# A written order for TensorE's projections and block products in a four-layer hybrid decoder trunk

## The chip, the cores and the metric

One core of a Trainium2 chip runs the whole network in one launch: 256 tokens, 1024 features, four layers, all in 32-bit floats. The metric is the device time of that launch in microseconds. The core has five engines that run side by side, each with its own in-order queue: TensorE (PE, with its weight loads PEld), VectorE (DVE), ScalarE (ACT), GpSimd (POOL) and SyncE (SP, which issues most DMAs).

## What is computed

Each layer is a half-weighted SwiGLU feed-forward network (FFN), a token mixer beside a memory attention, and a second FFN. The mixer is retention in layers 0 and 3, sparse attention with an indexer in layer 1, and native sparse attention in layer 2. Cut to what matters here:

```python
def swiglu(x, wg, wu, wd):
    return (jax.nn.silu(x @ wg) * (x @ wu)) @ wd     # wg, wu: 1024 x 2816, wd: 2816 x 1024

for i in range(DEPTH):
    h = rms_norm(x, ffn_norm[i, 0])
    x = x + 0.5 * swiglu(h, ffn_w_gate[i, 0], ffn_w_up[i, 0], ffn_w_down[i, 0])
    ...
    x = x + jnp.concatenate([y_mix, y_mem], axis=-1) @ w_out[i]
    h = rms_norm(x, ffn_norm[i, 1])
    x = x + 0.5 * swiglu(h, ffn_w_gate[i, 1], ffn_w_up[i, 1], ffn_w_down[i, 1])
```

## The kernel before

The tokens are two tiles of 128 rows (t = 0 and 1). Weights come from memory in units of 1 MB pieces (`raw`, three buffers). Every operand is split in two, a high half `hi` on ACT (line 264) and the rest `lo` on DVE (line 265), into nine slots each (`HALVES`), and one product is three matmuls: high by high, high by low, low by high. `mm3` (lines 290 to 294) writes these three. `project` (line 296) makes a projection from eight groups of them; half way through it calls `tick` (line 310), which splits some more weights and runs what is due. Delayed pieces, such as the transposes of the hidden activations `h` (`turn`, lines 1259 to 1264), are handed to `later` (line 348) with a number of ticks.

An FFN has eleven gate-and-up units and six down units, in the order of `FFN_ORDER`: g0 to g3, d0, g4, g5, d1, g6, g7, d2, g8, g9, d3, g10, d5, d4. A gate-and-up unit gives `pg`, from it `h`, and from its transposed halves (`hTh`, `hTl`) and the down weights the sums `acc`, over the whole FFN in four banks.

Units 4 and 5 go together, and so do 8 and 9: `joint` (line 460) computes their four block products for both token tiles with seven instead of eight, on sums and differences of weights (`t1` to `t4`; `b11`, `b21`, `b22` are plain) and of activations. Three PSUM banks A, B (both named `pg`) and C (`pj`) take them. There are 16 such blocks: two in each of eight FFNs. Of their seven products the last three and the vector work around them matter below:

```python
product(B, both("s3"), "t3", False)          # fourth
nc.vector.tensor_add(s3, B, s1)              # L493: reads bank B
product(A, half(1), "b21", False)            # fifth
chains[0].send((A, n0))                      # activation of A
nc.vector.tensor_sub(s3, C, s3)              # L496: reads bank C
product(B, both("a22"), "t4", False)         # sixth: adds to bank B
nc.vector.tensor_add(s1, B, s1)              # L498
chains[1].send((s1, n0)); chains[1].send((s3, n0))
product(C, both("s4"), "b22", False)         # seventh: adds to bank C
```

Behind a block stands the next down unit, d1 or d3, for tile 0 and then tile 1. [...]

Of the kernel before, what the change touches and what calls it, by code (L numbers as in the profile page):

```python
# [80 lines left out]
class Net:  # L81
    def __init__(self, ctx, tc, a, layers):
        self.tc, self.nc, self.a = tc, tc.nc, a
        self.layers = layers

        def pool(name, **k):
            return ctx.enter_context(tc.tile_pool(name=name, bufs=1, **k))

        self.cp, self.wp, self.ap, self.sp = pool("const"), pool("weights"), pool("act"), pool("small")
        self.ps = pool("psum", space=PSUM)  # L90
        self.units, self.raw, self.parts = [], {}, {}
        self.n_fetch = self.n_split = 0
        self.seq, self.due, self.queue, self.memkv = [], [], [[], []], {}
        self.ticks = 0
        self.jobs, self.open = [], []
        self.extra = []
        self.st, self.splits = [{}, {}], []
        self.plan()
# [188 lines left out]
        self.split()  # L287


    def mm3(self, out, ah, al, bh, bl, start, stop):  # L290
        mm = self.nc.tensor.matmul
        mm(out, ah, bh, start=start, stop=False)  # L292
        mm(out, ah, bl, start=False, stop=False)  # L293
        mm(out, al, bh, start=False, stop=stop)  # L294
# [53 lines left out]
    def later(self, n, fn, t=None):  # L348

        todo = [fn]  # L350

        def once():
            while todo:
                todo.pop()()

        self.due.append((n, once, t))
        return once
# [102 lines left out]
    def joint(self, u, chains):  # L460

        nc = self.nc
        while self.extra:
            self.extra.pop(0)()
        parts, ops = self.parts[u], self.ops
        s0 = self.st[0]["s"]
        both = lambda n: (ops[n][:, 0], ops[n][:, 1])
        half = lambda b: (s0[0][:, 4 * b:4 * b + 4], s0[1][:, 4 * b:4 * b + 4])

        def product(bank, a, name, first):  # L470
            mm = nc.tensor.matmul
            for k in range(4):
                bh, bl = [x[:, k % 2 * 512:k % 2 * 512 + 512] for x in parts[name][k // 2]]
                mm(bank, a[0][:, k], bh, start=first and k == 0, stop=False, skip_group_check=True)
                mm(bank, a[0][:, k], bl, start=False, stop=False, skip_group_check=True)
                mm(bank, a[1][:, k], bh, start=False, stop=k == 3, skip_group_check=True)
                if k == 1:
                    self.tick()

        n0 = self.st[0]["n"]  # L480
        A = self.pB("pg")
        product(A, half(0), "b11", True)
        s1 = self.t2([128, 512], "s1")
        nc.scalar.activation(s1, A, AF.Copy)
        B = self.pB("pg")
        product(B, both("s2"), "t2", True)
        s2 = self.t2([128, 512], "s2")
        nc.vector.tensor_add(s2, B, s1)
        C = self.bank("pj", "C")
        product(C, both("s1"), "t1", True)  # L490
        product(B, both("s3"), "t3", False)
        s3 = self.t2([128, 512], "s3")
        nc.vector.tensor_add(s3, B, s1)  # L493
        product(A, half(1), "b21", False)
        chains[0].send((A, n0))
        nc.vector.tensor_sub(s3, C, s3)  # L496
        product(B, both("a22"), "t4", False)
        nc.vector.tensor_add(s1, B, s1)  # L498
        chains[1].send((s1, n0))
        chains[1].send((s3, n0))  # L500
        product(C, both("s4"), "b22", False)
        nc.vector.tensor_sub(s2, C, s2)
        chains[0].send((s2, n0))
# [1090 lines left out]
```

## Time and profile before

| | before |
|---|---|
| median of the 3 runs shown | 2109.56 us (2107.13 to 2119.91) |
| profiled execution | 2109.68 us |
| its span in the trace | 2107.9 us |
| PE busy | 2028.5 us, 96% |
| DVE busy | 1520.9 us, 72% |
| ACT busy | 1114.2 us, 53% |
| POOL busy | 227.7 us, 11% |
| mean granted clock of TensorE | 0.985 |

The span runs from the first instruction to the last; 1.8 us lie around it. A busy PE is one with a matmul under way: matmuls overlap, so a row's duration is longer than the distance to the next row, and it is this distance that tells the rate. A row of a timeline ends, in brackets, with the idle time of its engine just before it and with what ended that.

### The profile page before, as it was taken

Reading aid. Unit: us, or ns where it says so; the run is one execution under the profiler, and the core shown is the slowest. Engines: PE = TensorE matmul, PEld = TensorE weight load, DVE = VectorE, ACT = ScalarE, POOL = GpSimd, SP = SyncE. Lnnn points to the kernel's source line nnn. Section 1 sums busy time; section 2 is a strip of 40 time slices with the busy share of each in tenths; the row PEclk is TensorE's granted clock in tenths of the full one; section 3 lists DMA queues with packets and bytes.
Section 4 is the critical chain, followed back from the end, with each engine's and each line's share of the span. In section 5 each row is a group of like instructions: output and inputs, shape, how many; then the busy total and the mean of one; then the engine's idle time right before and its main releaser. Section 6 shows DMA issues by size and latency. Waiting matters only on the chain.

```text
span 2107.9 us, 25369 instructions
## 1 busy us (share of the span) xinstructions
PE 2028.5 (96%) x9486; PEld 1628.5 (77%) x9486; DVE 1520.9 (72%) x2209; ACT 1114.2 (53%) x1562; POOL 227.7 (11%) x349
## 2 busy tenths in 40 slices
PE   8899999899989999989998999999899989999899
PEld 6677777778867887868777788877788778778687
DVE  7677757778767787867777876667786868658675
ACT  6455655446545555545545554544555545545453
POOL 0100411100100022100000112210000100301000
PEclk9999999999999999999999999999999999999999
DMA  7855535865683533684577443137744774436843
GB/s 260 261 189 220 180 120 200 241 218 200 213 245 143 205 110 120 234 246 145 218 235 242 182 173 130 64 121 235 241 179 180 231 248 181 159 120 215 249 149 126
DMA packets 66988, 402.11 MB, mean 191 GB/s; under 512 B 7600, under 2 KB 8016, under 8 KB 28080
## 3 DMA queue, kind: packets, MB, share of 16 engines
q1 hardware_dynamic: 56304, 364.54, 47.2%
q0 software_dynamic: 9408, 33.97, 8.3%
q10 hardware_dynamic: 1152, 1.97, 0.3%
q8 instruction: 75, 1.23, 0.2%
q14 instruction: 49, 0.40, 0.1%
HBM read 399.40 MB, written 1.05 MB: 190 GB/s over the span
## 4 chain that ended last, share of the span: by engine, by line
PE 74%; DMA 12%; DVE 8%; ACT 3%; issue 2%; POOL 1%; SPq 0%; ACTq 0%; DVEq 0%; POOLq 0%
PE pg L292 8%; PE pg L294 8%; PE pg L293 8%; PE acc L293 7%; PE acc L294 6%; PE acc L292 6%; DMA sum<-gu 5%; DVE lo L237 4%; DMA raw<-gu 3%; PE p L292 3%; DMA raw<-dn 3%; PE p L293 3%; PE p L294 3%; DVE lo L265 2%; PE pT L1262 2%
## 5 line engine op out<-in xcount | busy, mean ns | idle before, releaser
L265 DVE TENSOR_TENSOR lo<-raw,hi 128x1024 fp32r<-128x1024 f32 (+3 forms) x516 | 615.6, 1217 | 175.1 <-ACT hi L264 168.5
L264 ACT ACTIVATE hi<-raw 128x1024 fp32r<-128x1024 f32 (+3 forms) x516 | 527.1, 1046 | 273.0 <-DMA raw<-gu 79.0
L292 PE MATMUL pg<-hi,sh 128*128 128x512 f32 x896 | 354.8, 396 | 4.4 <-ACT hi L1347 3.4
L293 PE MATMUL pg<-lo,sh 128*128 128x512 f32 x896 | 350.7, 391 | 0.7 <-DVE lo L1348 0.7
L294 PE MATMUL pg<-hi,sl 128*128 128x512 f32 x896 | 349.8, 390 | 0.0
L292 PE MATMUL acc<-hi,hTh 128*128 128x512 f32 x704 | 286.0, 410 | 34.9 <-ACT hi L264 34.9
L293 PE MATMUL acc<-lo,hTh 128*128 128x512 f32 x704 | 288.0, 413 | 4.6 <-DVE lo L265 4.4
L294 PE MATMUL acc<-hi,hTl 128*128 128x512 f32 x704 | 282.4, 405 | 0.0
L236 ACT ACTIVATE hi<-sum 128x1024 fp32r<-128x1024 f32 x128 | 132.3, 1057 | 165.4 <-PE acc L294 88.9
L237 DVE TENSOR_TENSOR lo<-sum,hi 128x1024 fp32r<-128x1024 f32 x128 | 154.2, 1226 | 77.6 <-ACT hi L236 75.9
L292 PEld LDWEIGHTS pg<-hi,sh 128*128 128x128 f32 x896 | 168.3, 188 | 39.2 <-ACT hi L1347 4.3
L293 PEld LDWEIGHTS pg<-lo,sh 128*128 128x128 f32 x896 | 168.5, 188 | 35.4 <-DVE lo L1348 2.5
L294 PEld LDWEIGHTS pg<-hi,sl 128*128 128x128 f32 x896 | 168.2, 188 | 35.6 <-DVE sl L1370 0.4
L292 PEld LDWEIGHTS acc<-hi,hTh 128*128 128x128 f32 x704 | 135.8, 193 | 68.6 <-ACT hi L264 38.4
L293 PEld LDWEIGHTS acc<-lo,hTh 128*128 128x128 f32 x704 | 136.0, 193 | 42.0 <-DVE lo L265 14.2
L294 PEld LDWEIGHTS acc<-hi,hTl 128*128 128x128 f32 x704 | 136.4, 194 | 27.9 <-DVE hTl L1264 0.2
L1248 ACT ACTIVATE th<-pg,rh 128x256 f32<-128x256 f32 x128 | 60.3, 471 | 179.4 <-PE pg L294 174.0
L1249 DVE SCALAR_TENSOR_TENSOR th<-th,pg 128x256 f32<-128x256 f32 x128 | 53.5, 418 | 107.6 <-ACT th L1248 107.1
L237 DVE TENSOR_TENSOR lo<-raw,hi 128x1024 fp32r<-128x1024 f32 x96 | 114.9, 1226 | 18.9 <-ACT hi L236 18.9
L292 PE MATMUL p<-hi,sh 128*128 128x512 f32 (+4 forms) x320 | 125.2, 391 | 0.3 <-DVE dq_b L529 0.3
L294 PE MATMUL p<-hi,sl 128*128 128x512 f32 (+4 forms) x320 | 121.2, 379 | 0.0
L293 PE MATMUL p<-lo,sh 128*128 128x512 f32 (+4 forms) x320 | 120.9, 378 | 0.0
(344 smaller groups left out, 3185.0 us busy)
## 6 DMA issues: line engine op xcount, KB each, us to landing
raw<-gu SPq DMA_DIRECT2D x158, 1024.0 KB, 5.0
raw<-dn SPq DMA_DIRECT2D x88, 1024.0 KB, 4.9
sum<-gu SPq DMA_DIRECT2D x64, 512.0 KB, 7.6
sum<-gu POOLq DMA_DIRECT2D x64, 512.0 KB, 11.5
raw<-ret SPq DMA_DIRECT2D x20, 1024.0 KB, 4.8
raw<-wout SPq DMA_DIRECT2D x16, 1024.0 KB, 4.8
raw<-mkv SPq DMA_DIRECT2D x8, 1024.0 KB, 4.8
raw<-nsa SPq DMA_DIRECT2D x6, 1024.0 KB, 4.9
```

Source lines behind the costliest of these rows:

```text
L236: nc.scalar.activation(hi, x, AF.Copy)
L237: nc.vector.tensor_sub(lo, x, hi.bitcast(F32))
L264: nc.scalar.activation(hi, src, AF.Copy)
L265: nc.vector.tensor_sub(lo, src, hi.bitcast(F32))
L292: mm(out, ah, bh, start=start, stop=False)
L293: mm(out, ah, bl, start=False, stop=False)
L294: mm(out, al, bh, start=False, stop=stop)
L1248: nc.scalar.activation(th, p[:, :256], AF.Tanh, scale=rh_)
L1249: nc.vector.scalar_tensor_tensor(th, th, 1.0, p[:, :256], op0=OP.add, op1=OP.mult)
L1262: nc.tensor.transpose(c[:, k], h[:, k * 128:k * 128 + 128], self.ident)
```

## The change

Every matmul of `mm3` and of `joint`'s products now goes through a new function `mm`, which makes it depend on the one written before it, on the same engine and without a semaphore. The pieces handed to `later` are issued behind the last such matmul. Other matmuls and all transposes that aren't handed to `later` have no such dependency. The number of instructions on each engine is the same.

```diff
@@ class Net
+        self.last = None
@@
+    def mm(self, out, a, b, **k):
+
+        self.nc.tensor.matmul(out, a, b, **k)
+        i = self.nc.cur_bb.bb.instructions[-1]
+        if self.last is not None:
+            self.tc.add_manual_dep(
+                i, self.last.name,
+                mybir.DependencyInfo(mybir.DependencyClass.NoSync, mybir.DependencyReason.DATA), reason="in order")
+        self.last = i
+
     def mm3(self, out, ah, al, bh, bl, start, stop):
-        mm = self.nc.tensor.matmul
+        mm = self.mm
@@ later
             while todo:
-                todo.pop()()
+                if self.last is None:
+                    todo.pop()()
+                    continue
+                with self.tc.issue_after(self.last):
+                    todo.pop()()
@@ joint
         def product(bank, a, name, first):
-            mm = nc.tensor.matmul
+            mm = self.mm
```

All matmuls of projections and products have one line in the changed kernel, L293, and lines below it have moved by 15 (L493 is L508 there).

The first place is PE behind the fifth product of the first block in layer 1's first FFN. `pg_4965` is bank A, `pg_4984` bank B, `pj_5003` bank C; `acc0_4858` and `acc1_4859` are the down sums of tile 0. Before:

```order
L474 MATMUL pg_4965<-hi_4943,sh0_4341 128x512
L475 MATMUL pg_4965<-lo_4944,sh0_4341 128x512
L476 MATMUL pg_4965<-hi_4943,sl0_4342 128x512
L292 MATMUL acc0_4858<-hi_4972,hTh_4794 128x512
L293 MATMUL acc0_4858<-lo_4973,hTh_4794 128x512
L294 MATMUL acc0_4858<-hi_4972,hTl_4795 128x512
L292 MATMUL acc0_4858<-hi_4991,hTh_4794 128x512
```

And in the changed kernel:

```order
L293 MATMUL pg_4965<-hi_4943,sh0_4341 128x512
L293 MATMUL pg_4965<-lo_4944,sh0_4341 128x512
L293 MATMUL pg_4965<-hi_4943,sl0_4342 128x512
L293 MATMUL pg_4984<-hi_4948,op_4645 128x512
L293 MATMUL pg_4984<-lo_4949,op_4645 128x512
L293 MATMUL pg_4984<-hi_4948,op_4645 128x512 x2
L293 MATMUL pg_4984<-lo_4949,op_4645 128x512
```

Before, 15 `acc` matmuls stood between the fifth product and the sixth; now the sixth (`pg_4984` with the halves 4948 and 4949 of `t4`) follows at once. The same 15 moved in 15 of the 16 blocks, and 16 in the very first.

The second place is PE at the end of the seventh product (`pj_5003`) of the same block. Before:

```order
L474 MATMUL pj_5003<-hi_4961,op_4737 128x512
L475 MATMUL pj_5003<-lo_4962,op_4737 128x512
L476 MATMUL pj_5003<-hi_4961,op_4737 128x512
L292 MATMUL acc1_4859<-hi_4991,hTh_4794 128x512
L293 MATMUL acc1_4859<-lo_4992,hTh_4794 128x512
L294 MATMUL acc1_4859<-hi_4991,hTl_4795 128x512
L292 MATMUL acc1_4859<-hi_5010,hTh_4794 128x512
```

And in the changed kernel:

```order
L293 MATMUL pj_5003<-lo_4962,op_4737 128x512
L293 MATMUL pj_5003<-hi_4961,op_4737 128x512
L293 MATMUL acc0_4858<-hi_4972,hTh_4794 128x512
L293 MATMUL acc0_4858<-lo_4973,hTh_4794 128x512
L293 MATMUL acc0_4858<-hi_4972,hTl_4795 128x512
L293 MATMUL acc0_4858<-hi_4991,hTh_4794 128x512
L293 MATMUL acc0_4858<-lo_4992,hTh_4794 128x512
```

The down unit now begins here, with its first matmul; before it went on from its sixteenth.

The third place is DVE at the same block: the splits of the weights of `b22` (4957, 4961) and of the down unit (4972, 4991, 5010, 5026), and L493, which reads bank B. Before:

```order
L237 TENSOR_TENSOR lo_4958<-raw_4709,hi_4957 128x1024
L237 TENSOR_TENSOR lo_4962<-raw_4709,hi_4961 128x1024
L265 TENSOR_TENSOR lo_4973<-raw_4800,hi_4972 128x1024
L265 TENSOR_TENSOR lo_4992<-raw_4800,hi_4991 128x1024
L265 TENSOR_TENSOR lo_5011<-raw_4802,hi_5010 128x1024
L265 TENSOR_TENSOR lo_5027<-raw_4802,hi_5026 128x1024
L493 TENSOR_TENSOR s3_5036<-pg_4984,s1_4982 128x512
```

And in the changed kernel:

```order
L238 TENSOR_TENSOR lo_4958<-raw_4709,hi_4957 128x1024
L238 TENSOR_TENSOR lo_4962<-raw_4709,hi_4961 128x1024
L266 TENSOR_TENSOR lo_4973<-raw_4800,hi_4972 128x1024
L266 TENSOR_TENSOR lo_4992<-raw_4800,hi_4991 128x1024
L266 TENSOR_TENSOR lo_5011<-raw_4802,hi_5010 128x1024
L266 TENSOR_TENSOR lo_5027<-raw_4802,hi_5026 128x1024
L508 TENSOR_TENSOR s3_5036<-pg_4984,s1_4982 128x512
```

Nothing moved here. Elsewhere the difference is small: in layer 1's mixer the memory projections `pmkv`, the output projection `po` and the attention's small matmuls change places, with a few ACT and DVE instructions; in the first FFN one DMA issue on SP and one split each on ACT and DVE change places with a neighbour; and a few transposes of `h` and `x` stand one to four matmuls sooner or later.

## Rows read from the trace of the kernel before

**Rows 1.** The page: the span, and PE's busy time, share and instructions.
```profile
span 2107.9 us, 25369 instructions
PE 2028.5 (96%) x9486; PEld 1628.5 (77%) x9486; DVE 1520.9 (72%) x2209; ACT 1114.2 (53%) x1562; POOL 227.7 (11%) x349
```

**Rows 2.** Waits of PE: line, released by; us in total, times, longest.
```profile
PE acc L292 <- ACT hi L264: 34.9, 8, 5.7
PE pT L1262 <- DVE h L1254: 20.7, 15, 5.1
...
PE pT L674 <- POOL mk L669: 2.8, 3, 1.4
```

**Rows 3.** Timeline of PE, a first block: start, us, engine, line, operation, [idle before].
```profile
610.92 0.39 PE L476 MATMUL pg<-hi,sl 128*128 128x512 f32 x1
...
612.31 0.40 PE L294 MATMUL acc<-hi,hTl 128*128 128x512 f32 x1
618.19 0.80 PE L292 MATMUL acc<-hi,hTh 128*128 128x512 f32 x1 [5.48 <-ACT hi L264]
...
623.03 0.42 PE L474 MATMUL pg<-hi,op 128*128 128x512 f32 x1
...
628.42 0.39 PE L476 MATMUL pj<-hi,op 128*128 128x512 f32 x1
```

**Rows 4.** Timeline of DVE at the same block.
```profile
618.17 2.36 DVE L265 TENSOR_TENSOR lo<-raw,hi 128x1024 fp32r<-128x1024 f32 x2 [6.46 <-ACT hi L264]
620.44 0.69 DVE L493 TENSOR_TENSOR s<-pg,s 128x512 f32<-128x512 f32 x1
```

**Rows 5.** Timeline of ACT at the same block.
```profile
617.08 2.00 ACT L264 ACTIVATE hi<-raw 128x1024 fp32r<-128x1024 f32 x2 [7.37 <-DMA raw<-dn]
```

**Rows 6.** Timeline of DVE at the second block of the same FFN.
```profile
684.39 4.62 DVE L265 TENSOR_TENSOR lo<-raw,hi 128x1024 fp32r<-128x1024 f32 x4
688.94 0.68 DVE L493 TENSOR_TENSOR s<-pg,s 128x512 f32<-128x512 f32 x1
```

**Rows 7.** Timeline of PE at that second block.
```profile
685.80 0.39 PE L476 MATMUL pg<-hi,sl 128*128 128x512 f32 x1
...
689.88 0.40 PE L474 MATMUL pg<-hi,op 128*128 128x512 f32 x1
```

**Rows 8.** Timelines of DVE and PE at the very first block.
```profile
99.03 0.68 DVE L493 TENSOR_TENSOR s<-pg,s 128x512 f32<-128x512 f32 x1
99.78 0.50 PE L474 MATMUL pg<-hi,op 128*128 128x512 f32 x1
```

**Rows 9.** Busy time by stretch: PE, PEld, DVE, ACT, POOL, then PEclk, DMA, GB/s.
```profile
427.00:433.20 6.20, 6.20 (x25) 5.05 (x24) 3.99 (x4) 4.09 (x6) 0.00 (x0) 0.88 1.04 346
587.00:589.00 2.00, 0.02 (x1) 0.00 (x0) 1.98 (x4) 0.93 (x1) 0.00 (x0) 1.00 1.06 326
108.20:110.40 2.20, 0.01 (x1) 0.05 (x1) 2.20 (x5) 1.25 (x2) 0.00 (x0) 1.00 0.96 309
111.10:114.50 3.40, 3.40 (x11) 2.61 (x10) 2.60 (x5) 0.99 (x2) 0.00 (x0) 0.50 0.97 380
618.20:623.00 4.80, 4.33 (x9) 3.08 (x10) 4.25 (x6) 1.24 (x2) 0.86 (x1) 0.50 1.04 350
623.03:628.65 5.62, 5.62 (x26) 4.56 (x24) 4.07 (x4) 4.17 (x6) 0.00 (x0) 1.00 1.03 343
```

**Rows 10.** Timelines of DVE and PE at the last first block.
```profile
1991.92 0.68 DVE L493 TENSOR_TENSOR s<-pg,s 128x512 f32<-128x512 f32 x1
1994.50 0.63 PE L474 MATMUL pg<-hi,op 128*128 128x512 f32 x1
```

**Rows 11.** Timelines of DVE and PE at the last second block.
```profile
2060.88 0.68 DVE L493 TENSOR_TENSOR s<-pg,s 128x512 f32<-128x512 f32 x1
2061.83 0.39 PE L474 MATMUL pg<-hi,op 128*128 128x512 f32 x1
```

**Rows 12.** Timeline of PE, a wait of a transpose behind a first block.
```profile
634.62 0.44 PE L1262 MATMUL pT<-ident,h 128*128 128x128 f32 x2 [0.75 <-DVE h L1254]
```

## The prediction

> **What bounds the kernel now.** I began with the busy times on the page: TensorE (PE) is busy 96% of 2107.9 us [rows 1]. The kernel is bound by PE, so what counts is where PE idles and whether the new order puts idle time in. Its waits were read next: 34.9 us in 8 waits of a down projection (`acc`) for a high half from ScalarE (ACT), and 20.7 us in 15 waits of transposes for `h` [rows 2]. Then I looked up the order of the two kernels, and the timelines of PE, VectorE (DVE) and ACT at the 16 joint blocks, since nearly all that moves on PE is there: 15 `acc` matmuls in each block (16 in the very first) stood between the fifth product (`b21`) and the sixth (`t4`), and stand behind the seventh (`b22`) now. I call the two blocks of an FFN the first and the second block.
>
> In the first block of layer 1's first FFN [rows 3], `b21` ends with the matmul of 610.92, six `acc` matmuls follow at 0.232 us each ((612.31 - 610.92)/6), then PE idles 5.48 us for a high half of the down weights. `t4` starts at 623.03. It looks as if the `acc` matmuls held up two products that were ready.
>
> They were not. `t4` adds to bank B, whose old content L493 must read first (`s3 = B + s1`). DVE works in order, and L493 stands behind two splits of the same down weights, which start at 618.17 after 6.46 us of idle; L493 runs from 620.44 to 621.13 [rows 4]. The splits wait for the ACT half of 617.08, and that for the DMA of the weights [rows 5]. So `t4` could not have begun before 621.13, whatever stood ahead of it. In the second block of the same FFN nothing waits for a DMA, but DVE is busy with four splits from 684.39 on, and L493 runs from 688.94 to 689.62 [rows 6]; PE has ended `b21` with the matmul of 685.80 and fills the time until 689.88 with the 15 `acc` matmuls [rows 7]. They are cover for L493 in all 16 blocks.
>
> **The change part by part.** [...] DVE's order at the blocks stays, the L493 row included, and ACT's too, so the time at which L493 ends stays where it is relative to `b21`: the DMA, the splits and the slots that they need (given back by products up to `b21`) all lie ahead of the moved matmuls. What is queued behind the waiting `t4` on PE is `b22`, the 15 `acc`, the transposes of `h` and the next projection; the vector work that waits for these has its own slack there, or is priced below.
>
> How soon `t4` follows L493 is seen in the very first block, where nothing else held it: 99.03 + 0.68 = 99.71, start 99.78, so 0.07 us [rows 8].
>
> *First blocks.* `t4` starts at 621.13 + 0.07 = 621.20 instead of 623.03: -1.83 us. `t4` and `b22` took 5.62 us at the full clock [rows 9]. [...] Now PE waits nearly 10 us, and it is `t4` and `b22` that run at half rate for those 4.8 us: 2.4 us lost. They end at 629.2 instead of 628.65, +0.6. And the 15 `acc` matmuls are still to do: 15 x 0.232 = 3.5 us. Together +4.05. In four of the seven blocks the low clock already reached into `t4` (granted 0.88 over 427.00 to 433.20 [rows 9], some 0.75 us of loss), so I take 3.6 each. The last of the seven has the same shape: L493 ends at 1992.60, `t4` starts at 1994.50 [rows 10]. Seven blocks: 25.2 us.
>
> *The very first block* has `t4` at the same time as before, then 2.4 us for the clock and 16 x 0.232 = 3.7 us. Half of the 2.2 us in which PE waits for `h` afterwards (108.20 to 110.40 [rows 9]) may cover some of it. I take +5.0; its ends are +3.9 and +6.1.
>
> *Second blocks.* `t4` starts 0.07 us after 689.62, 0.2 us sooner than 689.88. The last block gives the same, 2061.56 against 2061.83 [rows 11]. Then 3.48 - 0.20 = 3.28 us are lost, eight times: 26.2 us. PE now idles some 3.5 us in each, as it never did there. Does the clock fall? A wait of 2.0 us left it at 1.00; one of 2.2 us was followed by 3.4 us at 0.50, which costs 1.7 us [rows 9]; all longer ones brought it down. Lower bound 0, upper bound what the first blocks pay, 2.4 to 2.9. Between them I take 1.7 us in three blocks of four: 1.3 each, 10.4 us.
>
> [...]
>
> *The rest.* In layer 1 the memory projections (`pmkv`), the output projection (`po`) and the small attention matmuls exchange places. PE has no wait of note there, and each order offers filler; the nearest row is 2.8 us in 3 waits of a transpose for POOL [rows 2], so within 3 us either way, taken as 0. In the first FFN one SP issue of a `sum` load goes ahead of one `raw` load, and one pair of DVE and ACT splits changes places with a neighbour. I take 0, covered by PE's projections; uncovered it costs at most the 5.1 us of the longest wait for `h` [rows 2]. A few transposes shift by one to four matmuls: 0.
>
> Sum: 25.2 + 5.0 + 26.2 + 10.4 = 66.8 us. On the profiled execution's 2109.7 us, which is the median of the runs within 0.2 us, that gives 2176.5 us.
>
> **The rivals.**
>
> *The waits go away (the other side).* If `t4` and `b22` were ready when `b21` ends, PE would run them in the 5.6 us in which the splits are made, and `acc` would find its halves ready. The 34.9 us would go [rows 2], and half of 4.8 us of low clock in seven blocks, 17 us: 2058 us. It decides if L493 ends before `b21` does in the first blocks, that is 9 us sooner than in [rows 4]. For it: the only large PE wait is the one that the moved matmuls make. Against it: `t4` 0.07 us behind L493 in [rows 8], and an unchanged order on DVE. Chance 0.04.
>
> *No change.* Either later idle time takes up the 3.5 us per block, or PE runs matmuls behind a waiting one. For the first: 79 us of idle in all (2107.9 - 2028.5), of which 44 are not the `acc` waits. But they are waits for `h`, which is made from these very products, so they move along. Against the second: PE idled 0.75 us for a transpose at 634.62 while ready `acc` matmuls stood behind it [rows 12]. Time 2110 us, chance 0.05. [...]
>
> *The clock holds in the second blocks.* 66.8 - 10.4: 2166 us, chance 0.13. For it: the 2.0 us wait at 1.00.
>
> *The clock falls in all of them and stays down as in the first blocks.* 8 x 2.9 = 23 instead of 10.4: 2190 us, chance 0.18.
>
> **How the numbers follow.** The forecast, with part of the second blocks at half clock, has 0.60: 2176.5 us. Four cases of five lie between 2150 and 2198: the lower end is a clock that holds in the second blocks and some 16 us of cover found in waits for `h`, the upper end the last rival plus 5 us for layer 1 and longer low clocks in the first blocks. A measurement of this kernel tells about 1%, 21 us, from no change; faster 0.04, same 0.05, slower 0.91 from the cases above.
>
> **What would show it.** Right: in PE's waits the line of `acc` for ACT is gone, and a new line of the block product for DVE, the line of `s3 = B + s1`, holds about 100 us in 16 waits, near 10 us in seven of them, 6 in one and 3.4 in eight; the granted clock falls in the blocks; PE's busy time changes little but for the half clock. Wrong step by step: `t4` starting well before that DVE instruction ends (the dependency isn't there); PE not idle in the second blocks (other cover exists); idle time behind the blocks shrinking by as much as was put in (cover later on).

## The result, and the profile after

The changed kernel takes 2180.75 us (median of 4 runs, 2173.58 to 2184.93) against 2110.21 us of the kernel before in the same session (2107.13 to 2119.91): ratio 1.0323, 95% interval 1.0279 to 1.0367, slower. The forecast was 2176.5 us in a range of 2150 to 2198, with a chance of 0.91 for slower. The profiled execution is the longest of the four, 2184.93 us.

The page of the changed kernel: the span, PE's busy time and the group of matmuls that waits most (busy, mean ns of one, idle time before them and its releaser). Of the lines named further on, 264 and 265 are 265 and 266 now, 496 is 511 and 1254 is 1269.

```profile
span 2183.2 us, 25398 instructions
PE 2041.4 (94%) x9486; PEld 1642.7 (75%) x9486; DVE 1522.0 (70%) x2209; ACT 1114.4 (51%) x1562; POOL 226.4 (10%) x349
...
L293 PE MATMUL pg<-hi,op 128*128 128x512 f32 x384 | 151.8, 460 | 100.4 <-DVE s L508 100.4
```

PE's waits in the changed kernel (total us, times, longest):

```profile
PE pg L293 <- DVE s L508: 100.4, 16, 11.3
PE pT L1277 <- DVE h L1269: 21.4, 13, 4.8
PE pT L689 <- POOL mk L684: 2.8, 3, 1.4
```

Against [rows 1] the span grew by 75.3 us and PE's busy time by 12.9, while the mean granted clock fell from 0.985 to 0.970. The 29 instructions more on the page are semaphore instructions, 16 on PE and 13 on ACT: the counts per engine are not quite the same, though the section on the change says so. Against [rows 2] the 34.9 us of `acc` for ACT are gone, and 100.4 us in 16 waits have come, one in each joint block, of the sixth product (`t4`) for `s3 = B + s1`.

The first block of layer 1's first FFN, as in [rows 3 to 5]. The timeline of PE in the changed kernel:

```profile
630.11 0.39 PE L293 MATMUL pg<-hi,sl 128*128 128x512 f32 x1
641.83 0.79 PE L293 MATMUL pg<-hi,op 128*128 128x512 f32 x1 [11.33 <-DVE s L508]
...
648.82 0.39 PE L293 MATMUL acc<-hi,hTh 128*128 128x512 f32 x1
```

DVE there:

```profile
638.82 2.36 DVE L266 TENSOR_TENSOR lo<-raw,hi 128x1024 fp32r<-128x1024 f32 x2 [7.88 <-ACT hi L265]
641.09 0.68 DVE L508 TENSOR_TENSOR s<-pg,s 128x512 f32<-128x512 f32 x1
```

ACT there:

```profile
637.73 2.00 ACT L265 ACTIVATE hi<-raw 128x1024 fp32r<-128x1024 f32 x2 [8.80 <-DMA raw<-dn]
```

The addition ends at 641.77 and `t4` starts 0.06 us later. The chain is the one of [rows 4, 5]: a DMA, two halves on ACT, two on DVE, the addition. The `acc` matmuls that stood in this wait start at 648.82, behind `b22`.

The second block of the same FFN, as in [rows 6, 7]; the stretches at the end have the columns PE, PEld, DVE, ACT, POOL, granted clock, DMA share, GB/s. The timeline of PE:

```profile
710.25 0.39 PE L293 MATMUL pg<-hi,sl 128*128 128x512 f32 x1
714.12 0.79 PE L293 MATMUL pg<-hi,op 128*128 128x512 f32 x1 [3.48 <-DVE s L508]
...
722.40 0.39 PE L293 MATMUL acc<-hi,hTh 128*128 128x512 f32 x1
```

DVE there:

```profile
708.84 4.63 DVE L266 TENSOR_TENSOR lo<-raw,hi 128x1024 fp32r<-128x1024 f32 x4
713.38 0.69 DVE L508 TENSOR_TENSOR s<-pg,s 128x512 f32<-128x512 f32 x1
```

The stretches there:

```profile
713.09:719.92 6.83, 5.80 (x14) 4.54 (x15) 4.93 (x8) 2.39 (x3) 0.00 (x0) 0.50 0.74 302
719.92:722.40 2.48, 2.48 (x12) 2.02 (x11) 1.73 (x3) 1.96 (x3) 0.00 (x0) 1.00 0.73 241
```

Four splits stand ahead of the addition, PE idles 3.48 us, and all of `t4` runs at half clock (0.50 until 719.92; its twelve matmuls take 5.29 us). The two products, 714.12 to 722.40, take 8.28 us instead of 5.51.

The same stamps read in all 16 blocks, from the end of the fifth product (`b21`: the start of its last matmul + 0.23 us) to the first matmul of the next projection, as means in us:

| | `b21` to `t4` | `t4` and `b22` | then to the next projection | sum |
|---|---|---|---|---|
| 7 first blocks, before | 11.28 | 6.03 | 9.58 | 26.89 |
| after | 9.82 | 7.66 | 12.95 | 30.43 |
| 8 second blocks, before | 3.85 | 5.51 | 8.67 | 18.03 |
| after | 3.63 | 7.66 | 12.01 | 23.30 |
| very first block, before | 6.38 | 5.69 | 12.39 | 24.46 |
| after | 5.08 | 7.00 | 16.50 | 28.58 |

That is 24.8 us in the seven first blocks, 42.2 in the eight second ones and 4.1 in the very first: 71.1 of the 75.3 us. Of the other 4.2, 0.6 arise ahead of the first block, 1.6 between layer 0's two FFNs and 2.0 between layer 1's.

### The profile page after: what moved, and what is told of

It reads as the page before. It is cut to its first block, busy times and chain, and to the rows that moved or that the text cites. A ratio compares the mean times of both kernels' runs of the same rounds, so it can differ in the third digit from the quotient of the medians.

```text
span 2183.2 us, 25398 instructions
## 1 busy us (share of the span) xinstructions
PE 2041.4 (94%) x9486; PEld 1642.7 (75%) x9486; DVE 1522.0 (70%) x2209; ACT 1114.4 (51%) x1562; POOL 226.4 (10%) x349
## 4 chain that ended last, share of the span: by engine, by line
PE 66%; DVE 14%; DMA 13%; ACT 4%; issue 3%; POOL 1%; SPq 0%; ACTq 0%; DVEq 0%; POOLq 0%
PE pg L293 24%; PE acc L293 19%; PE p L293 8%; DVE lo L238 6%; DMA sum<-gu 5%; DVE lo L266 4%; PE po L293 4%; DMA raw<-gu 4%; DMA raw<-dn 3%; ACT hi L237 2%; PE pT L1277 2%; PE pmkv L293 1%; PE pT L562 1%; PE pj L293 1%; ACT hi L265 1%
## 5 line engine op out<-in xcount | busy, mean ns | idle before, releaser
L293 PE MATMUL pg<-hi,sh 128*128 128x512 f32 x1024 | 404.8, 395 | 3.5 <-ACT hi L1362 2.5
L293 PE MATMUL pg<-lo,sh 128*128 128x512 f32 x1024 | 400.8, 391 | 1.0 <-DVE lo L1363 0.9
L293 PE MATMUL pg<-hi,sl 128*128 128x512 f32 x1024 | 399.5, 390 | 0.0
L293 PE MATMUL acc<-lo,hTh 128*128 128x512 f32 x704 | 283.1, 402 | 0.0
L293 PE MATMUL acc<-hi,hTh 128*128 128x512 f32 x704 | 282.2, 401 | 0.5 <-ACT hTh L1278 0.5
L293 PE MATMUL acc<-hi,hTl 128*128 128x512 f32 x704 | 281.9, 400 | 0.0
L293 PE MATMUL pg<-hi,op 128*128 128x512 f32 x384 | 151.8, 460 | 100.4 <-DVE s L508 100.4
L293 PEld LDWEIGHTS pg<-hi,sh 128*128 128x128 f32 x1024 | 192.3, 188 | 43.8 <-ACT hi L1362 3.8
L293 PEld LDWEIGHTS pg<-lo,sh 128*128 128x128 f32 x1024 | 192.5, 188 | 40.8 <-DVE lo L1363 2.9
L293 PEld LDWEIGHTS pg<-hi,sl 128*128 128x128 f32 x1024 | 192.3, 188 | 40.9 <-DVE sl L1385 0.4
L293 PEld LDWEIGHTS pg<-hi,op 128*128 128x128 f32 x384 | 87.0, 226 | 128.6 <-DVE s L508 107.1
L293 PEld LDWEIGHTS acc<-hi,hTh 128*128 128x128 f32 x704 | 133.6, 190 | 29.6 <-ACT hTh L1278 1.8
L293 PEld LDWEIGHTS acc<-hi,hTl 128*128 128x128 f32 x704 | 133.5, 190 | 29.0 <-DVE hTl L1279 1.1
L293 PEld LDWEIGHTS acc<-lo,hTh 128*128 128x128 f32 x704 | 133.5, 190 | 28.2
L238 DVE TENSOR_TENSOR lo<-raw,hi 128x1024 fp32r<-128x1024 f32 x96 | 114.9, 1225 | 17.2 <-ACT hi L237 17.2
L293 PE MATMUL p<-hi,sh 128*128 128x512 f32 (+4 forms) x320 | 125.2, 391 | 0.3 <-DVE dq_b L544 0.3
```

The lines of the kernel that those rows point to most:

```text
L238: nc.vector.tensor_sub(lo, x, hi.bitcast(F32))
L293: self.nc.tensor.matmul(out, a, b, **k)
```

## Experiments: which part of the change

**Products free.** In the changed kernel the block products go back to unordered matmuls.

```diff
-            mm = self.mm
+            mm = nc.tensor.matmul
```

> The changed kernel, with the matmuls of the block products taken out of the written order (the projections stay in it, the delayed pieces stay behind them). The order on TensorE then has 13 of the 15 down-projection matmuls ahead of the sixth product again. Theory (the loss is made in the 16 joint blocks, by the sixth product waiting for the addition that reads bank B): the cover is back but for two matmuls, about 2110 us (2100 to 2122), and the line of 100 us of waits for that addition falls below 15 us. Rival (the loss comes from the ordered projections or the delayed pieces elsewhere): it stays near 2180 us.

Measured: 2119.89 us, ratio to before 1.0033 (1.0013 to 1.0053). Its waits of PE:

```profile
PE acc L293 <- ACT hi L265: 35.2, 8, 6.6
PE pT L1277 <- DVE h L1269: 28.7, 19, 5.3
```

No wait for the addition is left, and the wait of [rows 2] is back. The second blocks are 0.44 us longer than before, two `acc` matmuls of 0.23 us less cover; the first blocks 0.7 us on average.

**Later pieces free.** In the changed kernel the delayed pieces are called as before.

```diff
-                if self.last is None:
-                    todo.pop()()
-                    continue
-                with self.tc.issue_after(self.last):
-                    todo.pop()()
+                todo.pop()()
```

> The changed kernel, with the delayed pieces free to go ahead of the projection again, as before; all matmuls keep the written order. Theory (the joint blocks make the loss): 2180 us, within 8. Rival (the held-back pieces make it): about 2110 us. A small part may lie there: the stretches of the mixers in layers 0 and 1 account for 1.6 and 2.0 us of the loss, so 2176 would say that these pieces made them.

Measured: 2179.85 us, ratio 1.0321 (1.0281 to 1.0361), not to be told from the changed kernel. The wait is the same:

```profile
PE pg L293 <- DVE s L504: 99.1, 16, 10.4
```

So the delayed pieces make none of the loss that can be measured. Whether the 1.6 and 2.0 us of the mixers came from them stays open: in this run these stretches lost 0.2 and 1.2 us, and a single execution scatters by more than that.

**Only the products ordered.** Projections and delayed pieces are as before.

```diff
     def mm3(self, out, ah, al, bh, bl, start, stop):
-        mm = self.mm
+        mm = self.nc.tensor.matmul
```

> One part of the change alone: only the matmuls of the block products are in the written order; projections and delayed pieces are free as before. The order then has 15 down-projection matmuls ahead of the sixth product, as before. Theory (the loss comes of the order of products against the following projection, and needs both in one order): about 2110 us (2100 to 2120). Rival (the products' own order makes the loss): 2180 us.

Measured, in a single run: 2116.6 us, beside runs of the kernel before of 2106.12 to 2124.29; the blocks differ from those of before by 0.1 us in the sum over the seven first and 0.2 over the eight second ones, and the very first is 1.2 us shorter. Neither half of the order makes the loss of 70 us: products free left 8 us of it, most of it in the blocks, and this run lies within the spread of the kernel before. It takes products and the following down projection in one chain: only then do all `acc` matmuls stand behind the sixth product. With the products free 13 of the 15 stood ahead of it, in this run all 15.

## Experiments: what the sixth product waits for

**The reader done three times.**

```diff
-        nc.vector.tensor_add(s3, B, s1)
+        for _ in range(3):
+            nc.vector.tensor_add(s3, B, s1)
```

> The changed kernel, with the addition that reads bank B done three times over (the same sum into the same place). Theory (the sixth product starts when the last reader of bank B on VectorE has ended): it starts later by two additions of 0.6 us and by the few small instructions that come between them, 1.9 to 2.1 us in each of 16 blocks, so about 2211 us (2200 to 2218). Rival (the sixth product waits for its own operands or for the down weights, and the addition ends at that time by chance): 2180 us, within 5.

Measured: 2208.28 us (2204.89 to 2216.24), ratio 1.0462. The timeline of DVE in the second block of layer 1's first FFN of this kernel:

```profile
717.14 0.68 DVE L509 TENSOR_TENSOR s<-pg,s 128x512 f32<-128x512 f32 x1
717.75 0.41 DVE L1265 SCALAR_TENSOR_TENSOR th<-th,pg 128x256 f32<-128x256 f32 x1
718.07 0.68 DVE L509 TENSOR_TENSOR s<-pg,s 128x512 f32<-128x512 f32 x1
718.67 0.47 DVE L1270 SCALAR_TENSOR_TENSOR h<-th,r,pg 128x256 f32<-128x256 f32 x1
719.06 0.68 DVE L509 TENSOR_TENSOR s<-pg,s 128x512 f32<-128x512 f32 x1
```

PE there:

```profile
719.80 0.80 PE L293 MATMUL pg<-hi,op 128*128 128x512 f32 x1 [5.40 <-DVE s L509]
```

`t4` starts 0.06 us behind the third reader, 1.92 us later against `b21` than in the changed kernel: the rival, own operands, is out. The time came out as forecast, but not from 16 equal parts. The second blocks lost 17.5 us more, the first ones only 2.6, although `t4` came 1.2 us later there, and the rest arose between the blocks. Something else also sets the length of the first blocks. The next experiments show what.

**Bank B first.** The splits of the down weights are held until the reader of bank B has been issued; the reader of bank C stays behind four of them.

```diff
+        held, self.splits = self.splits, []
         A = self.pB("pg")
...
         nc.vector.tensor_add(s3, B, s1)
+        self.splits = held
+        with self.tc.issue_after(self.nc.cur_bb.bb.instructions[-1]):
+            self.split_some(4)
```

> The changed kernel, with the splits of the down weights held back on VectorE until the addition that reads bank B has been done; the next reader, of bank C, still stands behind four of them. Theory: the sixth product follows the fifth at once, and the wait moves to the seventh, which needs bank C. It is shorter by the length of the sixth product, 2.8 us in first blocks, and in second blocks 1.5 us with a clock that holds (2 us more): 8 x 2.8 + 8 x 3.5 = 50 us less than 2181, about 2130 us (2115 to 2150). Rival (the sixth product waits for something else than the splits): 2180 us.

Measured: 2133.23 us (2132.01 to 2134.24), ratio 1.0108 (1.0095 to 1.0121). Its largest line of PE's waits:

```profile
PE pj L293 <- DVE s L515: 61.4, 15, 8.2
```

The timeline of PE in its third block, at the seventh product:

```profile
431.22 0.76 PE L293 MATMUL pj<-hi,op 128*128 128x512 f32 x1 [8.19 <-DVE s L515]
```

`t4` follows `b21` at once in all 16 blocks, and the seventh product waits instead, for the reader of bank C. The first blocks gained 2.6 us each and the second 3.8, near the 2.8 and 3.5 that were expected. The splits ahead of the readers are the cause of the waits.

## Experiments: the half clock

**Idle matmuls in the waits.**

```diff
         product(A, half(1), "b21", False)
...
+        pw = self.bank("pw", "C")
+        for _ in range((20, 13, 30)[self.blocks if self.blocks < 2 else 2 - self.blocks % 2]):
+            self.mm(pw, self.warm[:, :128], self.warm, start=True, stop=True)
+        self.blocks += 1
```

> The changed kernel, with idle matmuls (their result is used by nothing) between the fifth and the sixth product of each joint block: 20 in the very first, 30 in the first block of the other FFNs, 13 in the second blocks. At 0.215 us each they last 4.3, 6.5 and 2.8 us, less than the waits of 4.9, 8.3 and 3.3 us that they stand in, so that they delay nothing. They keep TensorE from idling before the sixth product but for 0.5 us (1.8 to 5 us in first blocks). Theory (half of the half-clock stretches behind the waits is lost: 6.83/2 or 3.41/2 us in the second blocks, 10.24/2 or less in the first, about 32 us in all, 16 of them in second blocks): 2149 us, between 2145 and 2165 if the clock falls still in some first blocks. Rival (the clock behind the waits costs nothing, since what follows waits for other engines anyway): 2180 us.

The stretches of half clock in it are those of the changed kernel's trace: a granted clock of 0.50 for 10.24 us at each of the seven first blocks, for 6.83 us at four second blocks and for 3.41 at the other four.

Measured: 2170.36 us (2166.99 to 2182.92), ratio 1.027 (1.0224 to 1.0316): 10.4 us less than the changed kernel, a third of what was expected. The timeline of PE in the second block of layer 1's first FFN of this kernel:

```profile
705.25 2.98 PE L293 MATMUL pw<-warm 128*128 128x512 bf16 x12
708.88 0.50 PE L293 MATMUL pg<-hi,op 128*128 128x512 f32 x1 [0.65 <-DVE s L508]
```

The 13 idle matmuls, 12 of them in the trace, last 2.98 us from the first start to the last end, where 2.8 us was expected.

The stretch of its sixth and seventh product there:

```profile
708.88:714.50 5.62, 5.62 (x25) 4.62 (x26) 5.17 (x7) 3.97 (x5) 0.00 (x0) 1.00 0.83 311
```

In the second blocks the theory held: `t4` starts at the same time, the clock is at 1.00, and the eight blocks lose 27.1 us instead of 42.2. These 15.1 us are the price of the half clock there. In the seven first blocks nothing was gained (25.6 us lost against 24.8). In six of them the clock still fell; 2.6 to 4.3 us of the wait were left idle. But two blocks kept it, the very first and the last of the seven, and they are no shorter: 4.1 against 4.1 us lost, and 5.1 against 3.5. The timeline of PE in the last of the seven:

```profile
2056.81 0.50 PE L293 MATMUL pg<-hi,op 128*128 128x512 f32 x1 [1.57 <-DVE s L508]
...
2069.32 0.99 PE L1281 MATMUL pT<-ident,h 128*128 128x128 f32 x4 [4.17 <-DVE h L1273]
```

ACT there:

```profile
2060.61 2.01 ACT L265 ACTIVATE hi<-raw 128x1024 fp32r<-128x1024 f32 x2 [5.54 <-DMA raw<-gu]
```

The products run at full rate, and then PE waits 4.17 us for `h`. Halves that wait 5.54 us for a DMA stand ahead of it. In these two blocks the half clock would have cost nothing by itself: it lay beside a wait that was still to come. For the other six first blocks no run shows what it cost.

## Experiments: take the wait away

**Both banks first.** The splits are held until both readers, and ACT's function of bank A, have been issued; in the changed kernel and in the kernel before.

```diff
+        held, self.splits = self.splits, []
         A = self.pB("pg")
...
         chains[0].send((A, n0))
+        th = [i for i in nc.cur_bb.bb.instructions[first:] if i.engine == mybir.EngineType.Activation][0]
         nc.vector.tensor_sub(s3, C, s3)
+        self.splits = held
+        with self.tc.issue_after(nc.cur_bb.bb.instructions[-1]), self.tc.issue_after(th):
+            self.split_some(4)
```

> The changed kernel, with the splits of the down weights held back until both banks have been read and ScalarE has begun the block's next function. Theory (the one thing late is the splits ahead of the two readers): sixth and seventh product follow the fifth at once, the splits are made under them, and the waits of 100 us and most of the half-clock stretches go, those of the kernel before as well: 2060 us (2050 to 2080), since before had 34.9 us of such waits and 17 us of half clock. Rival (with the splits late, the down projection waits as long as the products did): 2110 us or more. Rival (the written order as such is dear): about 2180 us.

> The kernel before, with the same holding back of the splits and none of the change. The order around the blocks is then that of the changed kernel with the splits held. Theory (where the readers of the banks stand on VectorE decides, and the order of TensorE follows from it): 2060 us, within 10 of the changed kernel with the splits held. Rival (the written order has a gain of its own once the stall is away): over 10 us slower than that.

Measured: 2107.7 us on the changed kernel, ratio 0.9984 (0.9968 to 1.0000), and 2102.8 us on the kernel before, 0.9962 (0.9949 to 0.9975). The loss of the change is gone, but the 50 us below it did not come. The waits of PE for `h` in the changed kernel with both banks first:

```profile
PE pT L1283 <- DVE h L1275: 60.8, 16, 7.7
```

Those of the kernel before with both banks first:

```profile
PE pT L1268 <- DVE h L1260: 58.4, 17, 6.9
```

Sixth and seventh product now follow at once in all blocks, and the waits for `h` have grown from 20.7 us [rows 2] to 60. The timeline of ACT in the third block (the first of layer 0's second FFN) of the changed kernel with both banks first:

```profile
426.22 2.00 ACT L265 ACTIVATE hi<-raw 128x1024 fp32r<-128x1024 f32 x2 [4.28 <-DMA raw<-gu]
428.13 1.29 ACT L1269 ACTIVATE th<-s,rh 128x256 f32<-128x256 f32 x3
```

DVE there:

```profile
423.90 0.68 DVE L523 TENSOR_TENSOR s<-pj,s 128x512 f32<-128x512 f32 x1
```

PE there:

```profile
430.75 1.09 PE L1283 MATMUL pT<-ident,h 128*128 128x128 f32 x4 [5.21 <-DVE h L1275]
```

The stall moved from DVE's queue to ACT's: the function `th`, whose inputs had been ready since 424.6 (the end of L523 on DVE), stands behind a half that waits for its DMA. Is it the place in the queue, or are the weights late in any case?

**Halves last.** As the kernel before with both banks first; each later split is also put behind the block's last `th` on ACT and its last `h` on DVE (`self.hold` is these two instructions). One variant issues two splits early instead of four.

```diff
             while self.splits and (n > 0 or self.splits[0][0] <= upto):
-            self.splits.pop(0)[1]()
+            with contextlib.ExitStack() as e:
+                for i in self.hold:
+                    e.enter_context(self.tc.issue_after(i))
+                self.splits.pop(0)[1]()
```

> The kernel before, with the splits held back as in the kernel of 2102.8 us and, beyond that, every later split put behind the block's last function on ScalarE and behind its last use on VectorE. There PE waited 58.4 us for h, near 6 us in each of the seven first blocks, and ScalarE's function for h stood behind a half that waited 5.2 us for its DMA. Theory A (the place in ScalarE's queue makes the wait): the waits for h fall to some 20 us and the time to about 2070 us (2060 to 2085). Theory B (the arrival of the weights sets the pace of the first blocks, whatever stands where): PE waits as long for the next down weights instead, 2102 us, within 6.

> The same, with two splits of the down weights instead of four ahead of the block's functions. Theory A: the third and fourth half, which wait 2.3 to 4 us for their DMA, no longer stand ahead of the last uses of banks B and C either, so it is 2065 us or a little less than the run with four. Theory B: 2102 us; and it can be slower than that, to 2115, in the second blocks, where all four halves are there early and the down projection is made to wait for the two held ones.

Measured: 2059.34 us (2055.49 to 2068.89), ratio 0.9759 (0.9726 to 0.9792), faster than both kernels and just below the range of Theory A; with two splits early 2064.8 us, ratio 0.9781 (0.9755 to 0.9807), which can't be told from it. The largest line of PE's waits in the kernel of 2059 us:

```profile
PE pT L1275 <- DVE h L1267: 21.6, 15, 5.4
```

ACT in its third block:

```profile
423.73 1.31 ACT L1261 ACTIVATE th<-s,rh 128x256 f32<-128x256 f32 x3 [2.08 <-DVE s L509]
425.96 2.01 ACT L266 ACTIVATE hi<-raw 128x1024 fp32r<-128x1024 f32 x2 [0.92 <-DMA raw<-gu]
```

PE there:

```profile
425.64 0.85 PE L1275 MATMUL pT<-ident,h 128*128 128x128 f32 x6 [1.30 <-DVE h L1267]
```

The kernel before with both banks first, at the same place, first ACT and then PE:

```profile
427.77 2.00 ACT L264 ACTIVATE hi<-raw 128x1024 fp32r<-128x1024 f32 x2 [5.23 <-DMA raw<-gu]
432.31 1.09 PE L1268 MATMUL pT<-ident,h 128*128 128x128 f32 x4 [6.14 <-DVE h L1260]
```

The weights come no sooner: that half starts 12.2 us after `b21` (425.96 - 413.75), in the kernel of 2102.8 us 12.1 (427.77 - 415.63). But `th` runs ahead of it, and the transposes start 11.9 us after `b21` instead of 16.7. Seven first blocks gain 44.0 us on the kernel before, the very first 6.7, the second ones 2.6; 3.5 us of this are lost again outside the blocks. The place in the in-order queue made the wait.

**Without the accumulating transfers.** The kernel of 2102.8 us without the transfers that these two calls issue; it leaves a part of the computation out.

```diff
-        add("t1", b11)
...
-        add("t3", b22)
```

> The kernel of 2102.8 us, without the four accumulating transfers of 512 KB per joint unit that make the sums of weights (so the sums lack one term: this leaves a part of the computation out). The DMA engines are busy at a share of 1.0 throughout the first blocks. Theory B (the arrival of the weights sets the pace): 2 MB less to move per joint unit, 5 to 7 us at the 300 to 350 GB/s of those stretches, some of it ahead of the first blocks' weights: the waits for h fall by half or more, time 2060 to 2080 us. Theory A (the place in ScalarE's queue makes the wait, and the transfers are in time but for that): 2102 us, within 6.

Measured: 2018.6 us (2018.25 to 2022.68), ratio 0.9564 (0.9541 to 0.9587), below both theories. The waits for `h` are all but gone:

```profile
PE pT L1266 <- DVE h L1258: 1.5, 4, 0.7
```

ACT in its third block:

```profile
406.23 2.01 ACT L262 ACTIVATE hi<-raw 128x1024 fp32r<-128x1024 f32 x2 [1.03 <-DMA raw<-gu]
```

The weights come sooner here: that half starts 5.5 us after `b21` (406.23 - 400.74) instead of 12.1. The first blocks take 17.6 to 18.6 us from `b21` to the next projection, as long as the second ones (17.5). So Theory B was not wrong either: it needs both, weights that arrive late and a queue in which other work stands behind them. In the kernel of 2059 us the first blocks take 19.1 to 21.5 us; up to 4 us each are what late weights still cost. Some 20 of the 84 us against 2102.8 were gained outside the blocks, 7.5 of them ahead of the very first block and most of the rest behind second blocks; why was not followed up.

**The written order, with halves last.** The changed kernel with both edits.

> The changed kernel, written order and held pieces and all, with the splits held as in the kernel of 2059.3 us (ahead of them the readers of both banks, then the block's functions). Theory (the written order costs only where it meets a reader that stands late, and nothing by itself): 2059 us, between 2053 and 2068. Rival (the written order has a price of its own, as 2107.7 against 2102.8 us hinted with the splits held in one place only): 2064 to 2075 us, and more waits for h or for halves outside the blocks.

Measured: 2061.91 us (2061.11 to 2063.79), ratio 0.9762 (0.9737 to 0.9787), beside 0.9759 without the written order. The largest line of its waits of PE:

```profile
PE pT L1289 <- DVE h L1281: 23.2, 15, 5.1
```

The same order of matmuls that cost 3.2% costs nothing that can be measured once no reader is late. With both banks first alone a small price was left: 2107.7 against 2102.8 us, 0.2%, and nine of the twelve runs lie above all six of the other kernel. With halves last (2061.9 against 2059.3) the runs of the two overlap. What that price is made of stays open.

## Why the prediction was right, point by point

*The mechanism* was right at each step that it named: `t4` follows the addition by 0.06 us, the addition kept its place in DVE's order, PE runs nothing else in the wait, and the line of 100 us in 16 waits came as foretold (seven of 8.3 to 11.3 us, one of 4.9, eight of 3.3 to 4.3). That the addition also ends at the same time after `b21` held in the second blocks (3.58 us before and after, on average) and only roughly in the seven first ones (9.38 before, 9.76 after; from 1.2 us sooner to 1.6 us later in the single block), where it hangs on the DMA.

*First blocks:* 25.2 us forecast, 24.8 measured. The terms: `t4` sooner by 1.46 us instead of 1.83, clock 1.63 instead of 1.95 (3.6 + 1.83 - 3.48), `acc` 3.37 instead of 3.48. The 4.8 us of low clock behind the clock's term are the stretch from 618.20 on, at 0.50 [rows 9]; in the trace of the kernel before the clock was at 0.50 for 6.83 us at each of the seven waits of 4.25 to 5.71 us for a half. That the clock was a price there is in doubt all the same: with idle matmuls, the very first block and the last of the seven kept the clock and were no shorter, since the wait for `h` took what the clock would have taken. In these two blocks the sum was right by luck; for the other six it stays open.

*Very first block:* 5.0 forecast, 4.1 measured, inside its ends of 3.9 and 6.1. `t4` came 1.3 us sooner against `b21`, the half clock took 1.3 us instead of 2.4, and the rest grew by 4.1 us, 3.7 for `acc` and some wait for `h`.

*Second blocks:* the 3.28 us for lost cover were 3.13 (3.35 - 0.22). **The term that was mis-sized is their clock:** 1.3 us each, from three blocks of four at 1.7. It fell in all eight and cost 2.15 each, 17.2 us instead of 10.4. That is most of the gap between 66.8 and the 75.3 us of the profiled execution. The trace of the changed kernel has 0.50 behind all eight waits of 3.3 to 4.3 us; the section on what was unexpected has a block of another run that kept 1.00 through such a wait.

*The rest:* 0 was forecast with 3 us either way, 4.2 came in one execution. Its cause is not settled. The sum has no term for the dependencies themselves: with halves last the runs agree with that (2061.9 against 2059.3 us), with both banks first 0.2% is left.

*The rivals.* "The waits go away" was priced at 2058 us, with the condition that the addition ends before `b21` does. With both banks first the condition was met, and the time was 2102.8 and 2107.7 us. The step of it that fails is that the `acc` matmuls and `h` would find their inputs: the next wait, in ACT's queue, took nearly all of it. With that one gone too, the time was 2059.3. Of the two rivals on the clock, the one in which it holds came true in no second block of the profiled execution; the other had all eight fall, as they did, but at 2.9 us each.

## What to carry to other kernels

When PE idles in front of matmuls, ask what the work behind them waits for before moving it forward: matmuls in a gap may be its filler and not its cause. In an in-order queue, put short readers that give a PSUM bank or an input free ahead of work that waits for a DMA, on every engine of the chain; clearing one queue only moved the stall to the next (2110 to 2103 us), clearing both took 2.4% off. Price a half clock only where nothing later is waited for anyway: without it eight second blocks gained 15.1 us, the very first block and the last first block nothing.

## What was unexpected of the hardware

Waits of equal length were not followed by the same clock. In the changed kernel all eight second blocks, waits of 3.3 to 4.3 us, had a granted clock of 0.50 behind them. With the later pieces free, one of them kept 1.00 through a wait of 3.31 us and both products (stretches of that kernel, columns as above):

```profile
1610.40:1613.90 3.50, 0.19 (x2) 0.00 (x1) 3.50 (x5) 1.30 (x3) 0.00 (x0) 1.00 0.95 393
1613.90:1616.00 2.10, 2.10 (x9) 1.76 (x10) 2.10 (x4) 1.07 (x2) 0.00 (x0) 1.00 1.00 367
1616.00:1619.50 3.50, 3.50 (x17) 2.85 (x16) 3.05 (x4) 2.94 (x4) 0.00 (x0) 1.00 0.75 276
```

That block lost 3.3 us, where the seven others of the same execution lost 4.5 to 6.0. Nor did the longer wait always bring the clock down: in this execution a wait of 1.98 us (to 1509.27) was followed by 0.50, one of 2.21 us (to 2060.17) was not.

And the clock fell without any wait, in layer 2's mixer, in 6 of the 14 executions that were traced. In five of them it was at 0.50 for 3.4 us, so in the kernel before:

```profile
1369.00:1374.00 5.00, 5.00 (x38) 4.44 (x37) 1.47 (x2) 2.85 (x5) 0.00 (x0) 1.00 0.60 210
1374.00:1377.40 3.40, 3.40 (x12) 2.71 (x12) 2.50 (x10) 1.33 (x2) 0.49 (x1) 0.50 0.24 53
```

In the kernel with idle matmuls it stayed down for 23.9 us, from 1373.21 on, and PE was busy for the whole 5 us in each of these stretches:

```profile
1365.00:1370.00 5.00, 5.00 (x43) 4.88 (x43) 2.46 (x6) 4.11 (x9) 0.00 (x0) 1.00 0.01 3
...
1375.00:1380.00 5.00, 5.00 (x23) 4.46 (x22) 1.64 (x10) 1.16 (x3) 0.33 (x1) 0.50 0.54 200
...
1390.00:1395.00 5.00, 5.00 (x20) 3.89 (x20) 2.15 (x7) 0.70 (x1) 0.00 (x0) 0.50 0.61 213
```

The records show no cause: the same matmuls stand in the mixer of the eight other traces, at a granted clock of 1.00. The stretch between the two blocks around this mixer took 8.9 us longer in that execution than in the changed kernel, most of the 12.6 us by which it is longer than the median of its kernel.
